# Prefetch depth of a three-chunk product, and the order of its last group and stores

## The chip, the cores and the metric

The kernel runs on one core of a Trainium2 chip. The metric is the device time of one execution in microseconds: 1948.6 us, the median of three runs (1947.58 to 1950.29).

## The reference

One decoder layer on 512 tokens of width 2048, all in float32. The part around the change is the last line, a SwiGLU block of hidden width 5632 and the residual:

```python
    h2 = rms_norm(x, norm2_g[l])
    x = x + (jax.nn.silu(h2 @ w_gate[l]) * (h2 @ w_up[l])) @ w_down[l]
```

Ahead of it the layer has a combined projection, gated linear attention on four heads, dilated attention on eight heads, and an output projection.

## The kernel before

Every large product is computed with Strassen's scheme in Winograd's form on blocks of 256: four quarters a, b, c, d of a 512-row slab of the weights, seven products P1, P5, P6, P3, P7, P2, P4 in that order, each with one of seven combinations of the activation (A11, S1, S2, S4, S3, A12, A22). A product over a group of 512 rows of the weights is an item of the loop in `stream` (L380), called a group below. Each operand is kept as a high part, rounded to the matmul's type by ScalarE, and a low part, the rest, subtracted by VectorE. So a group is twelve matmuls (L398): eight with the weights' high part `wh` (the activation's high and low part, two halves jj of the rows, two halves m of the output rows) and four with the low part `wl`. The two halves m go to two accumulators `acc`. `wh` is cast by ScalarE (L371), `wl` by VectorE (L375), each one group ahead in two buffers; the sums of weight quarters are VectorE's too (L296).

The down product takes the gated activation's 22 blocks in three chunks i = 0, 1, 2 of four, four and three groups of rows. For each chunk there are two column pairs (np_ = 0, 1), each with 7 x 4 or 7 x 3 groups. Chunk 0 adds to `x1_d`, the others to `y_d`, in DRAM; chunk 2 stores to the output. This is `final_down`: the closing sums are made by VectorE (L334), then `residual` loads the rows to be added into the two tiles q and k (L1235) and adds them (L1240, or L1237 where the accumulator itself is still the source, as for the last two tiles of a pair).

The activation's parts of the next chunk are split while the second column pair of the chunk before runs. `down_jobs` makes the list of parts (28, or 21 for the last chunk) in the order of the products, each a load of 256 KB from `p_d` (a gated block, transposed) or from `sums_d` (sums of such blocks, printed S_d) into a tile, and a split into a tile of `apool`: a copy by ScalarE (L196) and a subtraction by VectorE (L197). `staged` keeps a number of loads ahead of the split in hand, and each step of the pair, one per group, splits one part. `fetch_part` gives the loads the tiles v, T, qT and kT in turn. The tiles oT and PT hold, until the end of the layer's gate and up product, the transposed gated tiles on their way to `p_d`.

Most loads and stores are issued by SP, which works through its queue in order and waits there for what an entry needs. The order of that queue is not that of the code: a scheduler places each instruction by when it expects its operands. TensorE, VectorE and ScalarE are each in order as well.

Of the kernel before, what the change touches and what calls it, by code (L numbers as in the profile page):

```python
# [14 lines left out]
ALU = mybir.AluOpType  # L15
# [3 lines left out]
P = 128  # L19
# [112 lines left out]
def block_kernel(ctx: ExitStack, tc: tile.TileContext, ins, out):  # L132
    nc = tc.nc
# [18 lines left out]
    def nm(s):  # L152
        uid[0] += 1
        return f"{s}_{uid[0]}"
# [7 lines left out]
    def work(tag, shape=(P, 512), bufs=1):  # L162
        return mp.tile(list(shape), F32, name=nm(tag), tag=tag, bufs=bufs)
# [6 lines left out]
    load = nc.sync.dma_start  # L170
    store = nc.sync.dma_start
# [88 lines left out]
    def folded(w):  # L260

        return w.rearrange("p (b a) -> p a b", b=2)

    def unfolded(t):

        return t.rearrange("p (a b) -> p b a", b=2)

    def halves(t):
        return t.rearrange("p (b a) -> p b a", b=2)
# [88 lines left out]
    def stream(pairs):  # L358


        items = [(p, prod, g) for p in pairs for prod in PRODUCTS for g in range(p.op.groups)]
        last = len(items) - 1
        sources, high, low = {}, {}, {}

        def total(k):
            p, prod, g = items[k]
            sources[k] = p.source(prod, g)

        def first_part(k):
            high[k] = hpool.tile([P, 2, 512], F32R, name=nm("wh"), tag="wh")  # L370
            nc.scalar.copy(high[k], sources[k])  # L371

        def second_part(k):
            low[k] = hpool.tile([P, 2, 512], F32R, name=nm("wl"), tag="wl")
            nc.vector.tensor_tensor(  # L375
                low[k], sources.pop(k), high[k].bitcast(F32), op=ALU.subtract
            )

        yield total, first_part, second_part
        for k, (p, prod, g) in enumerate(items):  # L380
            if g == 0:
                if prod == "P1" and p.before:
                    p.before()
                p.begin(prod)
            run_soon()
            if k < last:
                first_part(k + 1)
            if k + 2 <= last:
                total(k + 2)
            if k < last:  # L390
                second_part(k + 1)
            a = p.op.t[COMBO[prod], g]
            fresh = prod in ("P1", "P5", "P2")
            for w, terms in ((high.pop(k), (0, 1)), (low.pop(k), (0,))):
                for jj in range(2):
                    for m in range(2):
                        for hl in terms:
                            nc.tensor.matmul(  # L398
                                p.dst[prod][m], a[:, jj, hl, m * P : (m + 1) * P], folded(w[:, jj, :]),
                                start=fresh and g == 0 and len(terms) == 2 and jj == 0 and hl == 0,  # L400
                                stop=g == p.op.groups - 1 and len(terms) == 1 and jj == 1,
                                skip_group_check=not fresh,
                            )
                if len(terms) == 2:
                    p.step()
            if g == p.op.groups - 1:
                p.end(prod)
# [7 lines left out]
    def run_soon():  # L415
        for d in list(soonest):
            d[0] -= 1
            if d[0] <= 0:
                soonest.remove(d)
                d[1]()  # L420
# [267 lines left out]
    for g in range(4):  # L688
        for b in (2 * g, 2 * g + 1):
            if g < 2:  # L690
                t = apool.tile([P, 2, 512], F32, name=nm("xT"), tag="A")
# [342 lines left out]
    order = (2, 3, 0, 1)  # L1034
# [92 lines left out]
    def staged(items, ahead=1):  # L1127

        queue = []
        for key, fetch, use in items:  # L1130
            while key is not None and key not in done:
                if queue:
                    t, u = queue.pop(0)
                    u(t)
                yield
            queue.append((fetch(), use))
            if len(queue) > ahead:
                t, u = queue.pop(0)
                u(t)
                yield  # L1140
        for t, u in queue:
            u(t)
            yield

    tags = ("v", "T", "qT", "kT")
    count = [0]

    def fetch_part(src, half):
        def fetch():
            t = work(tags[count[0] % 4], (P, 2, 256))  # L1150
            count[0] += 1
            load(t, src[half])
            return t

        return (id(src), half), fetch
# [74 lines left out]
    def residual(tiles, acc_, rows, c0, src):  # L1230

        res = []
        for m in range(2):
            r = work(("q", "k")[m])
            load(r, src(rows[m], c0))  # L1235
            if tiles is None:
                nc.vector.tensor_tensor(halves(r), unfolded(acc_[m]), halves(r), op=ALU.add)  # L1237
                res.append(r)
            else:
                nc.vector.tensor_tensor(tiles[m], tiles[m], r, op=ALU.add)  # L1240
                res.append(tiles[m])
        return res
# [121 lines left out]
    def sums_job(j):  # L1364
# [19 lines left out]
        put("S4", v)  # L1384
        yield

    opd = [Operand(4), Operand(4), Operand(3)]

    def down_jobs(i):

        op = opd[i]
        items = []
        for prod in PRODUCTS:
            name = COMBO[prod]
            for g in range(op.groups):
                j = 4 * i + g
                if name in SUMS:
                    src = (sums_d[j][name], 0)
                else:
                    src = (p_d[2 * j + (name != "A11")], int(name == "A22"))  # L1400
                items.append(
                    (*fetch_part(*src), lambda t, name=name, g=g: op.split(name, g, t))
                )
        return staged(items, 2)

    paces = {0: [1, 1, 1, 1, 0, 0, 0, 0, 0, 0, 1, 1, 1, 1, 0, 0, 0, 0], 10: [0] * 6}
    def before_ffn(j):
        if j == 0:
            finish(lambda: ("A11", 3) in opn.t)
        elif j == 10:  # L1410
            background.append(down_jobs(0))
# [10 lines left out]
    def final_down(i, np_):  # L1422
        def final(half, which, tiles, acc_):
            rows = [2 * half, 2 * half + 1]
            c0 = 512 * (2 * np_ + which)
            prev = x1_d if i == 0 else y_d
            tiles = residual(tiles, acc_, rows, c0, lambda t, c: prev[t][:, c : c + 512])
            for m in range(2):
                t = rows[m]
                if i == 2:  # L1430
                    store(out[t * P : (t + 1) * P, c0 : c0 + 512], tiles[m])
                else:
                    store(y_d[t][:, c0 : c0 + 512], tiles[m])

        return final

    for i in range(3):
        g0 = 4 * i
        rows_d = [(512 * (g0 + g), 512 * (g0 + g) + 256) for g in range(opd[i].groups)]
        for np_ in range(2):  # L1440
            lead = np_ == 1 and i < 2
            pair(
                opd[i], rows_d, w_down[:, 2 * np_], w_down[:, 2 * np_ + 1],
                final_down(i, np_), paced([0] * 6) if lead else step,
                before=(lambda i=i: background.append(down_jobs(i + 1))) if lead else None,
            )

    rest = stream(pairs)
    begin = next(rest)
    with tc.manual_schedule(engines=ordered):  # L1450
# [57 lines left out]
```

## Time and profile before

| What | Value |
|---|---|
| median of the runs | 1948.6 us (1947.58 to 1950.29) |
| the profiled execution, own time | 1952.11 us |
| its span, first to last instruction | 1950.0 us |
| granted TensorE clock, mean | 0.998 |
| TensorE busy | 1916.9 us (98%) |
| VectorE busy | 1647.6 us (84%) |
| ScalarE busy | 1088.9 us (56%) |
| DMA, mean over the span | 178 GB/s |

Rows of the trace in order of time give the start in us from the span's start, the length, the engine (PE is TensorE, PEld its weight loads, DVE VectorE, ACT ScalarE, SPq the issue of a DMA by SP), the line, the operation, what is written and read by the program's names, and how many instructions of that kind stand together. Brackets give the idle time ahead of the row and what ended it. Ends of matmuls are modelled. Rows of windows give the stretch, the busy time and count for PE, PEld, DVE, ACT and POOL, the granted clock, the share of the DMA engines and GB/s. Rows of DMA issues end with the size of one and the median time to landing.

### The profile page before, as it was taken

The numbers are of one execution on the slowest core, as the hardware profiler recorded it, in microseconds if no ns is written. First come the engines' busy times: TensorE is split into PE (matmuls) and PEld (weight loads), VectorE is DVE, ScalarE is ACT, GpSimd is POOL, SyncE is SP. The second block draws the span as 40 slices with busy tenths as digits, with TensorE's granted clock in tenths as the row PEclk, the third lists the DMA queues.
The fourth block names the chain that finished last, engine by engine and source line by source line (L and its number), as shares of the span: only waits on it lengthen the run. The fifth ranks groups of instructions, "written<-read, shape, count | busy, mean of one in ns | idle before, by whom it ended". The sixth has DMA issues, their size and how long they took to land.

```text
span 1950.0 us, 25512 instructions
## 1 busy us (share of the span) xinstructions
PE 1916.9 (98%) x9160; PEld 1660.6 (85%) x9160; DVE 1647.6 (84%) x1845; ACT 1088.9 (56%) x1580; POOL 47.2 (2%) x73
## 2 busy tenths in 40 slices
PE   7999999999999999999999999999999999999998
PEld 6788888887888888888888888888888888888887
DVE  7996877767799999878878878878879989989987
ACT  8654564566676675544544544544546646546443
POOL 0000230001000000000000000000000000000000
PEclk9999999999999999999999999999999999999999
DMA  9445555454535563454464454453555765855662
GB/s 354 170 151 205 171 189 154 149 164 150 176 138 186 184 224 117 138 178 162 135 189 148 144 184 137 155 184 121 171 172 180 270 217 177 292 195 180 235 216 76
DMA packets 150791, 347.84 MB, mean 178 GB/s; under 512 B 15542, under 2 KB 42463, under 8 KB 150664
## 3 DMA queue, kind: packets, MB, share of 16 engines
q1 hardware_dynamic: 150520, 346.21, 53.5%
q8 instruction: 71, 1.16, 0.2%
q14 instruction: 56, 0.46, 0.1%
q10 hardware_dynamic: 144, 0.01, 0.0%
HBM read 288.20 MB, written 60.31 MB: 179 GB/s over the span
## 4 chain that ended last, share of the span: by engine, by line
PE 72%; DVE 7%; DMA 3%; issue 2%; ACT 1%; SPq 0%; POOLq 0%; POOL 0%; DVEq 0%; ACTq 0%
PE acc L398 68%; DVE wl L375 3%; PE bank L1059 1%; DVE wa L296 1%; PE bank L944 1%; PE bank L968 1%; DVE AS L197 1%; DMA wc<-in_w_in 0%; DMA p_d<-PT 0%; PE bank L935 0%; PE bank L961 0%; ACT wh L371 0%; DMA r<-p_d 0%; ACT jk L1019 0%; DMA q<-in_x 0%
## 5 line engine op out<-in xcount | busy, mean ns | idle before, releaser
L398 PE MATMUL acc<-wh,AS 128*128 128x512 f32 x3008 | 711.1, 379 | 0.0
L398 PEld LDWEIGHTS acc<-wh,AS 128*128 128x128 f32 x3008 | 568.6, 189 | 81.1 <-ACT wh L371 0.4
L371 ACT CAST wh<-wa 128x1024 fp32r<-128x1024 f32 x376 | 394.2, 1049 | 397.8 <-PE acc L398 357.7
L398 PE MATMUL acc<-wh,AA 128*128 128x512 f32 x2256 | 533.7, 379 | 2.8 <-ACT wh L371 2.8
L375 DVE TENSOR_TENSOR wl<-wa,wh 128x1024 fp32r<-128x1024 f32 x376 | 457.2, 1218 | 68.0 <-ACT wh L371 42.2
L398 PEld LDWEIGHTS acc<-wh,AA 128*128 128x128 f32 x2256 | 426.0, 189 | 64.5 <-ACT wh L371 4.0
L398 PE MATMUL acc<-wl,AS 128*128 128x512 f32 x1504 | 396.3, 385 | 3.9 <-DVE wl L375 3.8
L398 PEld LDWEIGHTS acc<-wl,AS 128*128 128x128 f32 x1504 | 280.1, 189 | 55.4 <-DVE wl L375 13.6
L398 PE MATMUL acc<-wl,AA 128*128 128x512 f32 x1128 | 295.1, 384 | 0.0
L398 PEld LDWEIGHTS acc<-wl,AA 128*128 128x128 f32 x1128 | 210.0, 189 | 29.8 <-issue 1.0
L371 ACT CAST wh<-wb 128x1024 fp32r<-128x1024 f32 x94 | 98.5, 1048 | 124.0 <-PE acc L398 118.4
L371 ACT CAST wh<-wc 128x1024 fp32r<-128x1024 f32 x94 | 98.5, 1047 | 110.8 <-PE acc L398 106.5
L371 ACT CAST wh<-wd 128x1024 fp32r<-128x1024 f32 x94 | 98.6, 1049 | 101.9 <-PE acc L398 93.3
L375 DVE TENSOR_TENSOR wl<-wc,wh 128x1024 fp32r<-128x1024 f32 x94 | 114.6, 1220 | 41.0 <-ACT wh L371 41.0
L375 DVE TENSOR_TENSOR wl<-wd,wh 128x1024 fp32r<-128x1024 f32 x94 | 114.4, 1219 | 38.9 <-ACT wh L371 30.1
L296 DVE TENSOR_TENSOR wa<-wc,wa 128x1024 f32<-128x1024 f32 x94 | 114.4, 1220 | 34.0 <-DMA wc<-in_w_gate 20.6
L375 DVE TENSOR_TENSOR wl<-wb,wh 128x1024 fp32r<-128x1024 f32 x94 | 114.1, 1217 | 4.8 <-ACT wh L371 4.5
L296 DVE TENSOR_TENSOR wa<-wb,wa 128x1024 f32<-128x1024 f32 x94 | 113.6, 1219 | 1.1 <-DMA wb<-in_w_in 0.4
L296 DVE TENSOR_TENSOR wb<-wd,wb 128x1024 f32<-128x1024 f32 x94 | 114.1, 1217 | 0.4
L296 DVE TENSOR_TENSOR wa<-wd,wa 128x1024 f32<-128x1024 f32 x94 | 113.0, 1217 | 0.8 <-DMA wd<-in_w_in 0.8
L338 DVE SCALAR_TENSOR_TENSOR seed<-acc,rs,seed 128x512 f32<-128x512 f32 x96 | 70.3, 745 | 27.8 <-PE acc L398 27.8
L322 ACT ACTIVATE seed<-acc,rs 128x512 f32<-128x512 f32 x96 | 60.7, 683 | 4.1 <-PE acc L398 4.1
(301 smaller groups left out, 1323.7 us busy)
## 6 DMA issues: line engine op xcount, KB each, us to landing
wa<-in_w_gate SPq DMA_DIRECT2D x44, 512.0 KB, 3.4
wb<-in_w_up SPq DMA_DIRECT2D x44, 512.0 KB, 4.4
wd<-in_w_up SPq DMA_DIRECT2D x44, 512.0 KB, 4.2
wc<-in_w_gate SPq DMA_DIRECT2D x44, 512.0 KB, 3.5
wc<-in_w_in SPq DMA_DIRECT2D x28, 512.0 KB, 3.5
wa<-in_w_in SPq DMA_DIRECT2D x24, 512.0 KB, 4.8
wb<-in_w_in SPq DMA_DIRECT2D x24, 512.0 KB, 5.9
wd<-in_w_in SPq DMA_DIRECT2D x24, 512.0 KB, 5.6
```

Of the source, the lines that this page charges most:

```text
L197: nc.vector.tensor_tensor(a[:, :, 1, :], src, a[:, :, 0, :].bitcast(F32), op=ALU.subtract)
L296: nc.vector.tensor_tensor(src, other, src, op=ALU.subtract)
L322: nc.scalar.activation(halves(t), unfolded(src[m]), AF.Copy, scale=self.scale(half, m))
L338: nc.vector.scalar_tensor_tensor(halves(seed[m]), unfolded(src[m]), self.scale(half, m), halves(seed[m]), op0=ALU.mult, op1=ALU.add,)
L371: nc.scalar.copy(high[k], sources[k])
L375: nc.vector.tensor_tensor(low[k], sources.pop(k), high[k].bitcast(F32), op=ALU.subtract)
L398: nc.tensor.matmul(p.dst[prod][m], a[:, jj, hl, m * P : (m + 1) * P], folded(w[:, jj, :]), start=fresh and g == 0 and len(terms) == 2 and ...
L944: nc.tensor.matmul(lp[:, :n], qh[:, b * P : (b + 1) * P], kh[:, :n], start=True, stop=True)
L968: nc.tensor.matmul(op, vh[:, k, :], lgs[b][:, k * P : (k + 1) * P], start=(k == 0), stop=(k == b))
L1059: nc.tensor.transpose(bk[:, jj, m * P : (m + 1) * P], tiles[m][:, f : f + P], ident)
```

## The change

Three things are changed; the third has two parts.

1. For chunks 1 and 2 the parts are loaded into six tiles in turn (oT and PT besides the four), with four loads ahead of the split in hand and not two. Chunk 0 stays as it was.
2. In the last group of the program the twelve matmuls are sorted by the half m: all six of the first accumulator, then all six of the second.
3. The last two tiles of the output get their rows in tiles of their own (tag L, two buffers) and no longer in q and k. The second of them is added and stored in two halves of 256 columns; the first of these stores is issued by ScalarE.

```diff
@@ stream
-            for w, terms in ((high.pop(k), (0, 1)), (low.pop(k), (0,))):
-                for jj in range(2):
-                    for m in range(2):
-                        for hl in terms:
-                            nc.tensor.matmul(
-                                p.dst[prod][m], a[:, jj, hl, m * P : (m + 1) * P], folded(w[:, jj, :]),
...
-                if len(terms) == 2:
+            w = high.pop(k), low.pop(k)
+            order = [(i, m, jj, hl) for i in range(2) for jj in range(2) for m in range(2)
+                     for hl in range(2 - i)]
+            if k == last:
+                order.sort(key=lambda o: o[1])
+            for n, (i, m, jj, hl) in enumerate(order):
+                nc.tensor.matmul(
+                    p.dst[prod][m], a[:, jj, hl, m * P : (m + 1) * P], folded(w[i][:, jj, :]),
...
+                if n == 7:
                     p.step()
@@ fetch_part
-    def fetch_part(src, half):
+    def fetch_part(src, half, tags=tags):
         def fetch():
-            t = work(tags[count[0] % 4], (P, 2, 256))
+            t = work(tags[count[0] % len(tags)], (P, 2, 256))
@@ down_jobs
+    wide = tags + ("oT", "PT")
...
-                    (*fetch_part(*src), lambda t, name=name, g=g: op.split(name, g, t))
+                    (*fetch_part(*src, tags if i == 0 else wide), lambda t, name=name, g=g: op.split(name, g, t))
...
-        return staged(items, 2)
+        return staged(items, 2 if i == 0 else 4)
@@ final_down
+            if i == 2 and np_ == 1 and tiles is None:
+                rs = [work("L", bufs=2) for _ in range(2)]
+                for m in range(2):
+                    load(rs[m], prev[rows[m]][:, c0 : c0 + 512])
+                for m in range(2):
+                    for b in range(1 if m == 0 else 2):
+                        c = slice(256 * b, 512 if m == 0 else 256 * b + 256)
+                        src, r = unfolded(acc_[m]), halves(rs[m])
+                        if m == 1:
+                            src, r = src[:, b], r[:, b]
+                        nc.vector.tensor_tensor(r, src, r, op=ALU.add)
+                        (nc.scalar.dma_start if m == 1 and b == 0 else store)(
+                            out[rows[m] * P : (rows[m] + 1) * P, c0 + c.start : c0 + c.stop],
+                            rs[m][:, c],
+                        )
+                return
```

What it moves, in the queues. SP's queue in the second column pair of chunk 0, before: loads of parts stand as v, T, qT, kT from S3_d (block 4 + g) and p_d, loads of weights as wa, the stores of a closed tile as y_d, and the loads of the rows for the next as q and k.

```order
L1152 DMA T_2607_14206<-S3_d5_201 128x512
L257 DMA wa_2628_14315<-in_w_down 128x1024
L1152 DMA qT_2611_14228<-S3_d6_205 128x512
L257 DMA wa_2633_14338<-in_w_down 128x1024
L257 DMA wa_2640_14363<-in_w_down 128x1024
L1433 DMA y_d0_222<-seed_2559_13979 128x512
L1433 DMA y_d1_223<-seed_2564_14002 128x512
L1235 DMA q_2605_14198<-x1_d2_142 128x512
L1235 DMA k_2606_14201<-x1_d3_143 128x512
L1152 DMA kT_2615_14250<-S3_d7_209 128x512
L1152 DMA v_2619_14273<-p_d9_165 128x512
```

The same place of SP's queue in the changed kernel:

```order
L1154 DMA PT_2609_14210<-S3_d7_209 128x512
L257 DMA wa_2630_14319<-in_w_down 128x1024
L1154 DMA v_2613_14232<-p_d9_165 128x512
L257 DMA wa_2635_14342<-in_w_down 128x1024
L257 DMA wa_2642_14367<-in_w_down 128x1024
L1452 DMA y_d0_222<-seed_2561_13983 128x512
L1452 DMA y_d1_223<-seed_2566_14006 128x512
L1237 DMA q_2607_14202<-x1_d2_142 128x512
L1237 DMA k_2608_14205<-x1_d3_143 128x512
L1154 DMA T_2617_14254<-p_d11_167 128x512
L1154 DMA qT_2621_14277<-p_d13_169 128x512
```

The load of S3_d7 stood behind the stores and the loads of q and k; it now stands ahead of them, in the slot that S3_d5 had, and every later part's load has moved up by two in the same way. In chunk 1's second column pair it is alike: there the load of p_d19 into kT (group 1 of A22) stood behind such stores and loads, and now stands two loads earlier. Where the six tiles start, SP's queue at the end of the gate and up product has a new entry: after the two stores of the last gated tile (p_d20 from oT, p_d21 from PT) the load of p_d8 into oT, and behind it the four loads of r for the last sums.

TensorE's last group (the names are the two accumulators, the weights' high and low part, and the activation's part), before:

```order
L398 MATMUL acc_2947_16022<-wh_3013_16405,AA22_2869_15569 128x512 x2
L398 MATMUL acc_2948_16023<-wh_3013_16405,AA22_2869_15569 128x512 x2
L398 MATMUL acc_2947_16022<-wh_3013_16405,AA22_2869_15569 128x512 x2
L398 MATMUL acc_2948_16023<-wh_3013_16405,AA22_2869_15569 128x512 x2
L398 MATMUL acc_2947_16022<-wl_3014_16407,AA22_2869_15569 128x512
L398 MATMUL acc_2948_16023<-wl_3014_16407,AA22_2869_15569 128x512
L398 MATMUL acc_2947_16022<-wl_3014_16407,AA22_2869_15569 128x512
L398 MATMUL acc_2948_16023<-wl_3014_16407,AA22_2869_15569 128x512
```

and in the changed kernel, with the row ahead of it:

```order
L400 MATMUL acc_2948_16023<-wl_3012_16390,AA22_2865_15548 128x512
L400 MATMUL acc_2947_16022<-wh_3013_16405,AA22_2869_15569 128x512 x4
L400 MATMUL acc_2947_16022<-wl_3014_16407,AA22_2869_15569 128x512 x2
L400 MATMUL acc_2948_16023<-wh_3013_16405,AA22_2869_15569 128x512 x4
L400 MATMUL acc_2948_16023<-wl_3014_16407,AA22_2869_15569 128x512 x2
```

The first accumulator is complete after the sixth matmul and not after the eleventh. The loads of the rows for the last two tiles, in the changed kernel's SP queue at the end of chunk 1 (out of the tiles q and k the stores to y_d, then the rows of the first tiles of chunk 2, and L the new ones):

```order
L1452 DMA y_d2_224<-q_2878_15610 128x512
L1452 DMA y_d3_225<-k_2879_15613 128x512
L1237 DMA q_2921_15865<-y_d0_222 128x512
L1433 DMA L_3017_16442<-y_d2_224 128x512
L1237 DMA k_2922_15868<-y_d1_223 128x512
L1433 DMA L_3018_16443<-y_d3_225 128x512
```

Before, those loads stood near the end of SP's queue, behind the last stores of closed tiles and ahead of the two final stores. On the other engines the order of all instructions is unchanged up to VectorE's last add, which is now two.

More of the change, by code (lines that the diff above doesn't have):

```diff
@@ L393, in stream @@
             fresh = prod in ("P1", "P5", "P2")
-            for w, terms in ((high.pop(k), (0, 1)), (low.pop(k), (0,))):
-                for jj in range(2):
-                    for m in range(2):
-                        for hl in terms:
-                            nc.tensor.matmul(
-                                p.dst[prod][m], a[:, jj, hl, m * P : (m + 1) * P], folded(w[:, jj, :]),
[L400 to L403, printed above, removed]
-                if len(terms) == 2:
+            w = high.pop(k), low.pop(k)
[6 more added lines that the diff above has]
+                    p.dst[prod][m], a[:, jj, hl, m * P : (m + 1) * P], folded(w[i][:, jj, :]),
+                    start=fresh and g == 0 and i == 0 and jj == 0 and hl == 0,
+                    stop=g == p.op.groups - 1 and i == 1 and jj == 1,
+                    skip_group_check=not fresh,
+                )
+                if n == 7:
                     p.step()
@@ L1426, in final @@
             prev = x1_d if i == 0 else y_d
+            if i == 2 and np_ == 1 and tiles is None:
[12 more added lines that the diff above has]
+                            rs[m][:, c],
+                        )
+                return
             tiles = residual(tiles, acc_, rows, c0, lambda t, c: prev[t][:, c : c + 512])
```

## The prediction

> **What bounds the kernel now.** I read the page first, then the instructions in order of time over the down product, then waits and windows. Its first part names TensorE:
>
> ```profile
> PE 1916.9 (98%) x9160; PEld 1660.6 (85%) x9160; DVE 1647.6 (84%) x1845; ACT 1088.9 (56%) x1580; POOL 47.2 (2%) x73
> ```
>
> So gains can only come from places where TensorE waits, and from what follows its last matmul. An undisturbed group of twelve matmuls takes 2.59 us from start to start (1665.68 to 1668.27 below). Twice in the down product a group starts over a microsecond late. TensorE at the first place (start, length; in brackets the idle time and what ended it):
>
> ```profile
> 1665.68 1.89 PE L398 MATMUL acc<-wh,AA 128*128 128x512 f32 x8
> 1668.27 1.89 PE L398 MATMUL acc<-wh,AA 128*128 128x512 f32 x8
> 1672.32 1.99 PE L398 MATMUL acc<-wh,AA 128*128 128x512 f32 x8 [1.25 <-ACT wh L371]
> ```
>
> The third group is due at 1668.27 + 2.59 = 1670.86; it starts 1.46 late and is 0.10 longer than the others: **1.56 us**. The other engines there:
>
> ```profile
> 1654.27 0.32 SPq L1152 DMA_DIRECT2D T<-S_d  x1
> 1664.88 0.43 SPq L1152 DMA_DIRECT2D kT<-S_d  x1
> 1669.79 1.28 DVE L334 TENSOR_TENSOR seed<-acc,seed 128x512 f32<-128x512 f32 x2
> 1670.70 0.62 ACT L196 CAST AS<-kT 128x512 fp32r<-128x512 f32 x1 [4.72 <-DMA kT<-S_d]
> 1670.99 0.68 DVE L1240 TENSOR_TENSOR seed<-seed,q 128x512 f32<-128x512 f32 x1
> 1672.30 1.23 DVE L375 TENSOR_TENSOR wl<-wc,wh 128x1024 fp32r<-128x1024 f32 x1 [0.62 <-ACT wh L371]
> 1680.65 0.63 ACT L196 CAST AA<-kT 128x512 fp32r<-128x512 f32 x1 [2.66 <-DMA kT<-p_d]
> ```
>
> ScalarE was free for the split of part kT at 1670.70 - 4.72 = 1665.98, but SP issued its load only at 1664.88, after the stores and loads that stand ahead of it in its queue, and it took 5.7 us. The cast for the next weights (wh) stands behind that split on ScalarE, so TensorE and VectorE waited for both. The second place is alike, in the next chunk:
>
> ```profile
> 1801.10 0.32 SPq L1152 DMA_DIRECT2D T<-p_d  x1
> 1815.10 1.89 PE L398 MATMUL acc<-wh,AA 128*128 128x512 f32 x8
> 1817.39 0.62 ACT L196 CAST AA<-kT 128x512 fp32r<-128x512 f32 x1 [4.59 <-DMA kT<-p_d]
> 1817.82 0.68 DVE L1240 TENSOR_TENSOR seed<-seed,q 128x512 f32<-128x512 f32 x1
> 1818.99 1.23 DVE L375 TENSOR_TENSOR wl<-wc,wh 128x1024 fp32r<-128x1024 f32 x1 [0.49 <-ACT wh L371]
> 1819.01 1.99 PE L398 MATMUL acc<-wh,AA 128*128 128x512 f32 x8 [1.12 <-ACT wh L371]
> 1829.89 1.22 DVE L375 TENSOR_TENSOR wl<-wa,wh 128x1024 fp32r<-128x1024 f32 x1 [0.85 <-ACT wh L371]
> ```
>
> Due at 1817.69, started at 1819.01, again 0.10 longer: **1.42 us**. The end of the program, with an earlier accumulator for comparison:
>
> ```profile
> 1935.82 1.03 PE L398 MATMUL acc<-wl,AA 128*128 128x512 f32 x4
> 1936.67 0.69 DVE L334 TENSOR_TENSOR seed<-acc,seed 128x512 f32<-128x512 f32 x1 [0.93 <-PE acc L398]
> 1940.20 1.22 DVE L375 TENSOR_TENSOR wl<-wa,wh 128x1024 fp32r<-128x1024 f32 x1
> 1940.71 0.45 SPq L1235 DMA_DIRECT2D q<-y_d  x1
> 1941.86 1.89 PE L398 MATMUL acc<-wh,AA 128*128 128x512 f32 x8
> 1943.59 1.03 PE L398 MATMUL acc<-wl,AA 128*128 128x512 f32 x4
> 1945.07 0.69 DVE L1237 TENSOR_TENSOR q<-acc,q 128x512 f32<-128x512 f32 x1 [3.64 <-DMA q<-y_d]
> 1945.80 0.69 DVE L1237 TENSOR_TENSOR k<-acc,k 128x512 f32<-128x512 f32 x1
> 1946.52 0.34 SPq L1431 DMA_DIRECT2D out<-k  x1
> SPq L1504 <- DMA out<-k: 2.0, 1, 2.0
> ```
>
> VectorE starts on a finished accumulator 0.18 before the modelled end of its last matmul (1936.85 against 1936.67), so the first closing add could start at 1943.59 + 1.03 - 0.18 = 1944.44. It starts at 1945.07, since its rows were loaded only at 1940.71. The last store, issued at 1946.52, has landed by 1946.86 + 2.0 = 1948.86 (the last row, from the waits of SP's queue); the span ends 1.14 later.
>
> **The change part by part.** Four parts ahead. TensorE's, VectorE's and ScalarE's orders stay as they were up to the last group; only SP's order moves, so nothing else is added to their queues. Each load takes the slot that the load of the part two before it had: at the first place S3_d7 goes out near 1654.27 and not at 1664.88, at the second p_d19 near 1801.10. By the 5.7 us above they land some 6 and 10 us before their splits. Next in danger is p_d11, now in the slot of 1664.88: landing about 1670.6, while its split is due two groups after 1665.98, at 1671.16. That is 0.5 us of cover; if it is gone, little is lost at first, since ScalarE's wait of 2.66 us at 1680.65 above held up no matmul. So both ScalarE waits go. What is late next is VectorE, which was busy without a break:
>
> ```profile
> 1644.94 1.22 DVE L375 TENSOR_TENSOR wl<-wd,wh 128x1024 fp32r<-128x1024 f32 x1
> 1646.21 1.13 PE L398 MATMUL acc<-wl,AS 128*128 128x512 f32 x4
> 1711.44 1.22 DVE L375 TENSOR_TENSOR wl<-wa,wh 128x1024 fp32r<-128x1024 f32 x1
> 1713.00 1.03 PE L398 MATMUL acc<-wl,AS 128*128 128x512 f32 x4
> 1716.87 1.23 DVE L375 TENSOR_TENSOR wl<-wd,wh 128x1024 fp32r<-128x1024 f32 x1 [0.81 <-ACT wh L371]
> ```
>
> Its low part (wl) ends at 1646.16, the four matmuls on it start 0.05 later and take 1.13 where others take 1.03: a late wl costs its lateness + 0.05 + 0.10. At the first place wl can follow the add of 1670.99 by one step of 0.60 (two adds take 1.28, of which 0.68 is the second): 1671.59 to 1672.81. TensorE wants it 1.73 after the group's start (1941.86 to 1943.59), at 1672.59. The loss is 0.22 + 0.15 = 0.37, the gain 1.56 - 0.37 = 1.19. From there VectorE runs 0.71 earlier than before (1671.59 for 1672.30) but TensorE 1.19, so every wl has 0.48 less room. The thinnest in that stretch is at 1713.00: wl ended at 1712.66, 0.34 ahead. It becomes 0.14 too late, a loss of 0.29. From 1716.87 VectorE waits for ScalarE again and nothing more is lost. First place: **0.90**. Second: wl at 1817.82 + 0.60 to 1819.64, wanted at 1817.69 + 1.73 = 1819.42, loss 0.37, gain **1.05**; VectorE is idle again by 1829.89. Bounds: nothing, if the loads are late again, to the full 1.56 and 1.42. I take the worked values, since VectorE's rows leave no other start.
>
> The six tiles add one wait: oT and PT still hold the last gated tile, so SP must see oT's store land before it loads p_d8 there; four loads of r, and the sums on VectorE, stand behind it.
>
> ```profile
> 1552.08 1.74 SPq L1122 DMA_DIRECT2D r<-p_d  x4
> 1558.01 1.22 DVE L375 TENSOR_TENSOR wl<-wa,wh 128x1024 fp32r<-128x1024 f32 x1
> 1559.88 1.03 PE L398 MATMUL acc<-wl,AS 128*128 128x512 f32 x4
> 1650.00:1672.00 22.00, 21.06 (x98) 17.75 (x96) 21.67 (x26) 10.96 (x15) 0.00 (x0) 1.00 0.92 304
> ```
>
> Those loads waited for PT's store, issued after oT's, already; added are one issue (1.74 / 4 = 0.44) and 256 KB on the DMA engines, 0.86 us at the 304 GB/s of the last row. VectorE may be up to 1.3 us late, against 0.65 of room in wl (1559.23 to 1559.88): a loss between 0 and 1.3 - 0.65 + 0.15 = 0.8. I take 0, since SP's old wait for PT's store covers the new one, and keep 0.8 for the range.
>
> The end. The rows' loads now go out behind the stores of the chunk before, two column pairs of 21 groups or 2 x 21 x 2.59 = 109 us earlier. With the last group sorted by row half, the first accumulator is done after six of its twelve matmuls, and its add (0.69) and store lie beside the other six. wl is ready at 1941.42 and is now wanted after four matmuls (4 x 1.73 / 8 = 0.86), at 1942.72. Six matmuls in a row go to one bank; sixteen did, at 1.8 / 15 = 0.12 us for half the columns, no slower than 0.216 for the whole:
>
> ```profile
> L741 PE MATMUL bank<-AS,gs x16: 274/281/283, 60.3 to 62.1; 128*128 128x256 f32 x16
> L834 DVE SCALAR_TENSOR_TENSOR L<-bank,L 128x256 f32<-128x256 f32 x4 | 1.6, 410 | 0.0
> ```
>
> The second accumulator is added in halves of 128x256, 0.41 us by the last row: 1944.44 to 1944.85, and 1944.77 to 1945.18. SP issues the last half 0.03 later, at 1945.21 for 1946.52: **1.31**. It lands and closes as before. Unsplit, the add would have ended at 1945.13, so the split gains nothing by itself; the first half's issue on ScalarE lies beside the second add. Bounds: 0.63 (the rows' load alone) to 1.37 (a split that costs nothing).
>
> [...]
>
> **Sum.** 0.90 + 1.05 + 1.31 = 3.26 us of the profiled execution, whose span is 1950.0 and own time 1952.11. The median of the runs is 1948.6, 3.5 below that; I take the same microseconds off it: **1945.3**.
>
> **The rivals.** First, VectorE keeps up (it finds slack that the rows hide): 1.56 + 1.42 + 1.31 = 4.29, 1944.3. Against it stand its rows without a gap. Second, the two waits are not there to be saved, because loads land sooner in runs without the profiler's traffic, or the moved loads are late in the stretch where the DMA engines are 0.92 busy: only the end is won, 1947.3. The 3.5 us between profile and median speak for it, two alike stalls in one execution against it. Third, slower: the first half's store goes by ScalarE's queue, unused since the program's start. If it lands as slowly as the slowest 256 KB store of the trace, the program's end waits for it:
>
> ```profile
> va<-seed SPq DMA_DIRECT2D x6, 256.0 KB, 8.2
> ```
>
> Issued at 1944.85 it lands at 1953.05, the end is 1954.19, and less 1.95 for the two places that is 2.2 slower: 1950.8. It decides once it takes longer than 1948.86 + 1.95 - 1944.85 = 6.0 us. Against it: the DMA engines are nearly idle then, and SP's last store took 2.34.
>
> **How the numbers follow.** My sum 0.45, VectorE keeps up 0.25, end only 0.20, ScalarE's store 0.06, other losses 0.04. About 0.2% or 3.9 us is what a measurement of this kernel can tell from no change, and my sum lies just inside. With 0.7 us of scatter on it, faster by more takes 0.20 of the second case and 0.14 of the first: 0.34; slower by more, half of the last two: 0.05; within: 0.61. The range leaves out most of the slow cases and reaches below the full gain by the scatter: 1943.2 to 1947.9.
>
> **What would show it.** Right: no group of the down product waits for ScalarE's split; the groups at the two places are 0.3 to 0.4 late after wl, not 1.3 to 1.5; one near 1711 is late by 0.3; the last store is issued 1945.21 - 1941.86 = 3.35 us after the last group's first matmul, not 4.66. Wrong: ScalarE waiting for p_d11 or its followers, VectorE waiting for r near 1556, or a program end that waits for ScalarE's store.

## The result

The changed kernel takes 1946.18 us (median of 14 runs, 1941.98 to 1950.16) against 1950.36 (14 runs, 1946.55 to 1953.33) before. The ratio is 0.9977 with a 95% interval of 0.9968 to 0.9985: 0.23% faster, or 4.5 us (2.9 to 6.2) of 1950. The forecast was 3.3 us, inside that interval. Ratios leave out one run of e5 (2885.76 us) and two of the kernel before beside it (2510.14 and 4119.75), far above all others. The profiled execution has an own time of 1947.03 and a span of 1945.25, 4.72 below the 1949.97 of before: 0.66 of it ahead of the down product (its first group starts at 1538.49 for 1539.15, where the change moves nothing; over all profiles below that start lies between 1536.9 and 1541.6), 2.62 in fewer waits of TensorE in the down product, 1.44 behind the last group's first matmul.

The first part of the changed kernel's page; TensorE is now busy for 99% of the span:

```profile
PE 1917.8 (99%) x9160; PEld 1662.6 (85%) x9160; DVE 1647.6 (85%) x1846; ACT 1088.5 (56%) x1580; POOL 47.7 (2%) x73
```

The first place in the changed kernel, in order of time (start, length; a bracket would give a wait and what ended it). The load of S3_d7 is now the one into PT:

```profile
1652.51 0.32 SPq L1154 DMA_DIRECT2D PT<-S_d  x1
1664.12 0.62 ACT L196 CAST AS<-PT 128x512 fp32r<-128x512 f32 x1
1669.23 0.68 DVE L1242 TENSOR_TENSOR seed<-seed,q 128x512 f32<-128x512 f32 x1
1669.39 0.62 ACT L196 CAST AA<-T 128x512 fp32r<-128x512 f32 x1
1669.83 1.22 DVE L375 TENSOR_TENSOR wl<-wc,wh 128x1024 fp32r<-128x1024 f32 x1
1671.10 1.13 PE L400 MATMUL acc<-wl,AA 128*128 128x512 f32 x4
1672.07 1.89 PE L400 MATMUL acc<-wh,AA 128*128 128x512 f32 x8
```

The load goes out at 1652.51 and the split of PT runs at 1664.12 with no bracket, so without a wait. Nor does the next in danger, p_d11 (T, at 1669.39), have one. VectorE's add ends, wl follows by 0.60, ends at 1671.05, and its matmuls start 0.05 later and take 1.13: the next group is 0.35 late, where one was 1.46 and the next 0.10 late before. Near 1703 and 1711, and at the second place:

```profile
1702.29 1.13 PE L400 MATMUL acc<-wl,AS 128*128 128x512 f32 x4
1710.24 1.13 PE L400 MATMUL acc<-wl,AS 128*128 128x512 f32 x4
1812.74 0.61 ACT L196 CAST AA<-oT 128x512 fp32r<-128x512 f32 x1
1815.77 1.21 DVE L375 TENSOR_TENSOR wl<-wc,wh 128x1024 fp32r<-128x1024 f32 x1
1817.04 1.13 PE L400 MATMUL acc<-wl,AA 128*128 128x512 f32 x4
```

The two rows of 1.13 make their next groups 0.11 and 0.18 late. At the second place the split of p_d19 (oT, 1812.74) does not wait, and the group behind 1817.04 is 0.35 late, for 1.42 before. The end:

```profile
1938.58 1.03 PE L400 MATMUL acc<-wh,AA 128*128 128x512 f32 x4
1940.08 0.69 DVE L1440 TENSOR_TENSOR L<-acc,L 128x512 f32<-128x512 f32 x1 [1.93 <-PE acc L400]
1940.74 0.59 PE L400 MATMUL acc<-wl,AA 128*128 128x512 f32 x2
1941.38 0.76 DVE L1440 TENSOR_TENSOR L<-acc,L 128x256 f32<-128x256 f32 x2 [0.60 <-PE acc L400]
1941.83 0.35 ACTq L1441 DMA_DIRECT2D out<-L  x1
1942.16 0.33 SPq L1441 DMA_DIRECT2D out<-L  x1
```

and from the waits of SP's queue there (total, times, longest):

```profile
SPq L1523 <- DMA out<-L: 1.6, 3, 0.7
```

The first accumulator's add lies beside the second's matmuls, the second's two half adds start 0.05 behind the last matmul, and the last store is issued 3.58 us after the last group's first matmul (4.66 before). SP's longest last wait for a store is 0.7, where it was 2.0, and the span ends 3.09 after the last issue (3.45 before). So of the 1.44 us of the end 1.08 come from the earlier issue and 0.36 from what follows it.

### The profile page after: what moved, and what is told of

Read it like the earlier page. It is cut to its first block, busy times and chain, and to the rows that moved or that the text cites. A ratio compares the mean times of both kernels' runs of the same rounds, so it can differ in the third digit from the quotient of the medians.

```text
span 1945.2 us, 25510 instructions
## 1 busy us (share of the span) xinstructions
PE 1917.8 (99%) x9160; PEld 1662.6 (85%) x9160; DVE 1647.6 (85%) x1846; ACT 1088.5 (56%) x1580; POOL 47.7 (2%) x73
## 4 chain that ended last, share of the span: by engine, by line
PE 82%; DVE 10%; issue 3%; DMA 3%; ACT 2%; SPq 0%; POOL 0%; POOLq 0%; DVEq 0%; ACTq 0%
PE acc L400 75%; DVE wl L375 3%; PE acc L463 1%; DVE wa L296 1%; PE bank L1061 1%; DVE AS L197 1%; PE bank L946 1%; PE bank L970 1%; DVE wl L515 1%; PE bank L463 0%; DMA wc<-in_w_in 0%; PE bank L937 0%; ACT wh L371 0%; PE bank L963 0%; DVE AS L209 0%
```

## The experiments

Each ratio is to the kernel before, run beside it on the same chip; e1, e2, e3 and e6 shared one chip and its runs of before, so did e4, e5, e8 and e9, and e10 to e13. Lateness means: by how much more than 2.59 us two groups of TensorE are apart. Groups are counted from 0, the down product's first. "Place 1" sums groups 49 to 68 (from about 1668 to 1717), "place 2" groups 105 to 110 (1815 to 1829), "start" the groups 30 to 47 at the start of chunk 0's second column pair, "rows" groups 135 to 146 (about 1890 to 1920), "end" is the time from the last group's first matmul to the end of the span.

| Profile | place 1 | place 2 | start | rows | end |
|---|---|---|---|---|---|
| before | 1.56 | 1.42 | 1.25 | 1.02 | 8.11 |
| e1, before again | 2.62 | 0.37 | 0.14 | 2.87 | 8.31 |
| e3, end alone | 4.54 | 1.40 | 0.15 | 2.65 | 6.63 |
| changed | 0.64 | 0.35 | 0.14 | 1.44 | 6.67 |
| e10, changed again | 0.62 | 0.35 | 0.53 | 1.58 | 6.62 |
| e2, parts alone | 0.63 | 0.34 | 0.14 | 2.29 | 8.64 |
| e6, two ahead | 0.64 | 0.34 | 0.14 | 2.10 | 6.65 |
| e4, unsplit | 0.63 | 0.34 | 0.47 | 2.50 | 6.86 |
| e5, rows alone | 0.64 | 0.34 | 0.15 | 1.92 | 7.62 |
| e8, more rows | 0.63 | 0.34 | 0.15 | 0 | 6.62 |
| e11, rows all | 0.63 | 0.34 | 0.14 | 0 | 6.67 |

**e1, the kernel before again** (no edit).

> The kernel before, once more, to see which of its waits come back in a second execution. If the two late splits are set by the order of SP's queue, ScalarE waits again for the loads of S3_d7 and p_d19 and two groups of the down product again start 1.3 to 1.5 us late; if they are chance, they are elsewhere or gone. The five groups that were 0.1 to 0.3 late between 1628 and 1650 follow a wait of VectorE of 1.01 for the rows in q, which the changed kernel's profile does not have: by chance it differs between executions, so at least one of the five places differs here; if the change removed it, all of them (1.25 us) come back. Time: the same as before, within 0.15%.

Measured: ratio 0.9995 (0.9985 to 1.0005).

```profile
1663.30 0.43 SPq L1152 DMA_DIRECT2D kT<-S_d  x1
1669.53 0.62 ACT L196 CAST AS<-kT 128x512 fp32r<-128x512 f32 x1 [5.17 <-PE acc L398]
1671.15 1.99 PE L398 MATMUL acc<-wh,AA 128*128 128x512 f32 x8 [1.71 <-ACT wh L371]
1810.92 0.44 SPq L1152 DMA_DIRECT2D kT<-p_d  x1
1815.70 0.62 ACT L196 CAST AA<-kT 128x512 fp32r<-128x512 f32 x1 [3.46 <-DMA kT<-p_d]
1817.34 2.00 PE L398 MATMUL acc<-wh,AA 128*128 128x512 f32 x8
```

Both late splits are there again, so they belong to the order of SP's queue; what they cost is not fixed. The first split runs 6.23 us after its load's issue and TensorE is 1.91 late (the split's bracket names TensorE, whose group had just ended; but in the other two profiles with four tiles the same split waits for the load, and in the changed kernel it runs before that group starts, so it was the load). A third split waits 3.51 us at 1690.69 and costs 0.44, and with 0.27 in two more groups it is 2.62 in all. At the second place the split runs 4.78 us after the load's issue and TensorE lost only 0.37. The 1.25 us of the "start" column did not come back: those were chance, and no part of the change (e10 and e4, with the change, have some of them).

**e2, the parts alone**

```diff
-            if k == last:
+            if False:
                 order.sort(key=lambda o: o[1])
...
-            if i == 2 and np_ == 1 and tiles is None:
+            if False:
```

> The first of the three changes alone (six tiles, four ahead). My sum: the two late splits are gone, VectorE's low part is 0.35 late at both places and 0.29 near 1711, so TensorE's waits fall by 1.95 us; the end stays at 8.1 us from the last group's first matmul to the end of the span. Time 0.10% below before. The rival that VectorE keeps up: 2.98 us, 0.15%. The rival that only the end is won: no change in time.

Measured: ratio 0.9987 (0.9977 to 0.9996), 0.13% or 2.5 us. The interval is no judge between my sum (0.10%) and the rival that VectorE keeps up (0.15%); it excludes no gain. The profile decides between the two: the lateness behind wl is there, at 0.34, 0.29 and 0.34.

**e3, the end alone**

```diff
-    wide = tags + ("oT", "PT")
+    wide = tags
...
-        return staged(items, 2 if i == 0 else 4)
+        return staged(items, 2)
```

> The second and third change alone (sorted last group, own rows, last tile in halves). My sum: from the last group's first matmul to the end of the span 1.3 to 1.5 us less than the 8.1 before, and the two late splits are there as before. Time 0.07% below before. If only the end is won by the change, this kernel has all of it: 0.23% below before.

Measured: ratio 0.9986 (0.9977 to 0.9995), 0.14% or 2.7 us; 0.23%, all of the change, is at the interval's end. The end takes 6.63. The first place is the worst of the three profiles with four tiles:

```profile
1665.59 0.51 SPq L1154 DMA_DIRECT2D kT<-S_d  x1
1672.53 0.62 ACT L196 CAST AS<-kT 128x512 fp32r<-128x512 f32 x1 [6.11 <-DMA kT<-S_d]
1674.15 3.59 PE L400 MATMUL acc<-wh,AA 128*128 128x512 f32 x8 [2.64 <-ACT wh L371]
1675.87 0.68 DVE L197 TENSOR_TENSOR AS<-kT,AS 128x512 fp32r<-128x512 f32 x1
```

Issued at 1665.59, the part is split only at 1672.53. The group starts 2.84 late and its eight matmuls take 3.59 for 1.89: half of them need the part's own low part, which VectorE, late too, subtracts at 1675.87. That is 4.54 us at one place, from one load whose split came 1.1 us later than in the first profile (6.94 after its issue, for 5.82).

**e6, six tiles, two ahead**

```diff
-        return staged(items, 2 if i == 0 else 4)
+        return staged(items, 2)
```

> The changed kernel with two loads ahead instead of four, but the six tiles kept. SP's order is then that of the changed kernel except for one load that moves by one entry, so if the place in SP's queue is what matters, the two late splits stay away and the time is that of the changed kernel (0.23% below before, within 0.1%). If the number of loads in hand matters, the splits are late again, two groups wait 1.3 to 1.5 us, and the time is about 0.07% below before.

Measured: ratio 0.9966 (0.9954 to 0.9979), from five runs. In the profile the two places are those of the changed kernel:

```profile
1671.70 1.13 PE L400 MATMUL acc<-wl,AA 128*128 128x512 f32 x4
1672.66 1.89 PE L400 MATMUL acc<-wh,AA 128*128 128x512 f32 x8
1818.60 1.46 PE L400 MATMUL acc<-wh,AA 128*128 128x512 f32 x6
```

So it is the six tiles that bring the loads forward. The number in hand changes nothing at the two places: it shifts the load in the code, but SP's order is set by when the tile comes free, and that order is the changed kernel's but for this one load. (The reverse, more in hand with four tiles, was not run; its SP order has the load of S3_d7 behind the stores as before.)

**e4, the last tile whole**

```diff
-                    for b in range(1 if m == 0 else 2):
-                        c = slice(256 * b, 512 if m == 0 else 256 * b + 256)
+                    for b in range(1):
+                        c = slice(0, 512)
...
-                        (nc.scalar.dma_start if m == 1 and b == 0 else store)(
+                        store(
```

> The changed kernel, with the last tile added and stored whole, by SP. My step says that the split into column halves gains nothing by itself: the whole add takes 0.69 and not 0.76 for two halves, so the last store is issued 0.05 to 0.1 us earlier, and from there to the end of the span it takes the same 3.0 us. By the size of the store, half the bytes should land sooner: then the end here is 0.3 us later than in the changed kernel (6.6 us from the last group's first matmul to the end). Time the same as the changed kernel's within noise; the profile decides.

Measured: ratio 0.9976 (0.9967 to 0.9985), which can't be told from the changed kernel's.

```profile
1940.93 1.03 PE L400 MATMUL acc<-wh,AA 128*128 128x512 f32 x4
1943.72 0.69 DVE L1438 TENSOR_TENSOR L<-acc,L 128x512 f32<-128x512 f32 x1 [0.60 <-PE acc L400]
1944.44 0.33 SPq L1439 DMA_DIRECT2D out<-L  x1
```

```profile
SPq L1521 <- DMA out<-L: 1.9, 1, 1.9
```

The last store is issued 3.51 after the last group's first matmul, 0.07 sooner than with the split, as my step had it; but it ends the span 3.35 later and not 3.09. SP waits 1.9 for it. A half store is over 0.26 sooner, so the split gains 0.2. The same holds over all profiles: 3.04 to 3.09 us from the last issue to the end of the span in the nine with a half store, 3.35 to 3.73 in the five with a whole one. So of the two expected values the one by the store's size is the nearer.

**e5, only the rows' tiles of the end**

```diff
-            if k == last:
+            if False:
                 order.sort(key=lambda o: o[1])
```

with e4's edit besides.

> Of the end only the rows' own tiles, loaded early: the last group in its old order, both tiles added and stored whole by SP. My lower bound: the first add starts 0.63 us earlier after the last group than before, since it no longer waits for its rows, and the end is 7.5 us after the last group's first matmul, between 8.1 before and 6.6 in the changed kernel. If the rows' wait were the whole of it, it would be 6.6 to 6.8.

Measured: ratio 0.9987 (0.9975 to 1.0000).

```profile
1942.17 1.89 PE L400 MATMUL acc<-wh,AA 128*128 128x512 f32 x8
1944.75 1.29 DVE L1438 TENSOR_TENSOR L<-acc,L 128x512 f32<-128x512 f32 x2 [3.01 <-PE acc L400]
```

The adds start 2.58 after the group (3.21 before): 0.63, the forecast's lower bound. The end takes 7.62. With e4 that divides the end: mean of the three profiles with the old end 8.35 (they lie between 8.11 and 8.64); own rows 0.73 less; the order by row half 0.76 less (7.62 to 6.86); the split 0.2 less.

**e8, own rows for two tiles more**

```diff
-            if i == 2 and np_ == 1 and tiles is None:
+            if i == 2 and tiles is None:
```

and the split and ScalarE's store kept to `np_ == 1`.

> The changed kernel, with own row tiles for the last two tiles of chunk 2's first column pair as well. In the changed kernel VectorE waits 1.69 us for q's rows at 1887.66 and four groups from 1893 to 1913 are 0.26, 0.50, 0.50 and 0.18 us late. If that wait is their cause, it goes and the four fall from 1.44 to at most 0.5 us, time 0.05% below the changed kernel. If VectorE's work there is too much anyway, they stay above 1.0.

Measured: ratio 0.9974 (0.9963 to 0.9984). The groups near 1893 are all on time in the profile. Their cause in the other profiles is one row, here of e1:

```profile
1891.19 0.69 DVE L1237 TENSOR_TENSOR q<-acc,q 128x512 f32<-128x512 f32 x1 [3.44 <-DMA q<-y_d]
1893.07 1.13 PE L398 MATMUL acc<-wl,AA 128*128 128x512 f32 x4 [1.15 <-DVE wl L375]
```

VectorE waits 3.44 us for q's rows and everything behind it, the next low part first, is late. In the nine profiles of the table without such tiles this add waits 1.59 (before) to 3.44 us (e1) and 1.0 to 2.9 us are late there, least and most in the same two; in the two with them nothing. (For the add of before and of e5 the bracket names TensorE; that the rows are the cause there is taken from the others.) The intervals of e4 and e8, from the same chip, overlap.

**e9, adds on GpSimd**

```diff
-    def residual(tiles, acc_, rows, c0, src):
+    def residual(tiles, acc_, rows, c0, src, eng=nc.vector):
...
-                nc.vector.tensor_tensor(tiles[m], tiles[m], r, op=ALU.add)
+                eng.tensor_tensor(tiles[m], tiles[m], r, op=ALU.add)
...
-            tiles = residual(tiles, acc_, rows, c0, lambda t, c: prev[t][:, c : c + 512])
+            tiles = residual(tiles, acc_, rows, c0, lambda t, c: prev[t][:, c : c + 512],
+                             nc.gpsimd if i < 2 and np_ == 1 else nc.vector)
```

> The changed kernel, with the adds of rows to closed sums in the second column pairs of chunks 0 and 1 on GpSimd, which is 2% busy, and not on VectorE. If VectorE is what binds at the two places now, the groups that are 0.35 late at 1672 and 1818 and the two of 0.11 and 0.18 near 1703 and 1711 are on time, 1.0 us less. If the low part is late for another reason (ScalarE's cast of the high part), they stay. A price may come with it: SP's stores of the sums wait for GpSimd, and with them the loads behind; if an add there takes over 3 us, splits get late again and the time is above the changed kernel's.

Measured: ratio 1.0002 (0.9992 to 1.0012). All of the gain is gone.

```profile
1661.03 1.29 POOL L1242 TENSOR_TENSOR seed<-seed,q 128x512 f32<-128x512 f32 x1 [1193.27 <-DMA v<-p_d]
1661.32 2.08 DVE L375 TENSOR_TENSOR wl<-wb,wh 128x1024 fp32r<-128x1024 f32 x1
1662.27 2.27 POOL L1242 TENSOR_TENSOR seed<-seed,k 128x512 f32<-128x512 f32 x1
1663.33 1.78 DVE L197 TENSOR_TENSOR AS<-T,AS 128x512 fp32r<-128x512 f32 x1
1665.62 1.21 DVE L296 TENSOR_TENSOR wa<-wc,wa 128x1024 f32<-128x1024 f32 x1
1666.76 1.21 DVE L375 TENSOR_TENSOR wl<-wb,wh 128x1024 fp32r<-128x1024 f32 x1
1668.03 1.13 PE L400 MATMUL acc<-wl,AS 128*128 128x512 f32 x4 [1.71 <-DVE wl L375]
```

VectorE's low part takes 2.08 beside the add on GpSimd (1.22 alone), its next subtraction 1.78 (0.68 alone), and TensorE waits 1.71 for a low part. Three groups at the first place and three at the second are 0.61, 1.97, 0.22 and 0.51, 1.97, 0.23 late. The time was lost, but not by the way that I named: no split waits for its load here. The order of VectorE's work has changed too: the scheduler has put a sum of weights (wa, 1665.62) ahead of the low part that is due (1666.76). e13 below has the same order on VectorE, ScalarE and TensorE without any add, and there these six groups are 1.25 late in all and not 5.5; so the order makes the group behind it late, but the loss against the changed kernel comes with the adds on GpSimd. Both lengths are roughly those of an instruction that has waited for the add beside it: 2.08 against 1.22 plus the 1.00 (1661.03 + 1.29 - 1661.32) that was left of the first add when the low part began, 1.78 against 0.68 plus the 1.21 (1662.27 + 2.27 - 1663.33) that was left of the second when the subtraction began. Why they would wait is not shown.

**e10, the changed kernel again** (no edit).

> The changed kernel once more, beside the three below on the same chip. If the loads are early enough in every execution, the two places read as in its first profile: one group 0.35 late near 1672, 0.29 in two groups near 1703 and 1711, one 0.35 late near 1818, and none waits for ScalarE there. The end takes 6.6 us from the last group's first matmul. The groups late near 1893 differ (they hang on the rows in q): 1.4 to 2.9 us. Time 0.23% below before, within 0.1%.

Measured: ratio 0.9980 (0.9970 to 0.9990); the two places within 0.02 of the first profile's, "rows" 1.58, the end 6.62.

**e11, own rows at every pair's end**

```diff
-            if i == 2 and np_ == 1 and tiles is None:
+            if tiles is None:
+                last = i == 2 and np_ == 1
...
-                            out[rows[m] * P : (rows[m] + 1) * P, c0 + c.start : c0 + c.stop],
+                            (out[rows[m] * P : (rows[m] + 1) * P, c0 + c.start : c0 + c.stop]
+                             if i == 2 else y_d[rows[m]][:, c0 : c0 + 512]),
```

and the split and ScalarE's store under `last`.

> The changed kernel, with own row tiles, loaded early, for the last two tiles of every column pair of the down product and not of the last alone. If late rows are what makes VectorE wait where a pair ends, the groups late near 1893 (1.4 to 2.9 us in the profiles so far) are all on time, and none of the groups from 1612 to 1645 is late (0 to 1.25 us); the 0.35, 0.29 and 0.35 stay. Time 0.05 to 0.15% below the changed kernel's. If VectorE's work there is too much by itself, the groups stay late by about 1.4 us and the time is the same.

Measured: ratio 0.9966 (0.9954 to 0.9979), seven runs, median 1946.47 beside 1948.60 for e10.

```profile
1886.87 0.68 DVE L1441 TENSOR_TENSOR L<-acc,L 128x512 f32<-128x512 f32 x1
1887.90 1.03 PE L400 MATMUL acc<-wl,AA 128*128 128x512 f32 x4
```

No bracket: the rows are there, and no group is late from 1890 on. With e8 that settles the cause of the "rows" column. "Start" is 0.14, as low as the best. This is the fastest version, by 2.1 us of medians; its interval and e10's still touch, so the time alone does not show it.

**e12, the half store by SP**

```diff
-                        (nc.scalar.dma_start if m == 1 and b == 0 else store)(
+                        store(
```

> The changed kernel, with the first half of the last tile stored by SP and not by ScalarE. By my step the issue on ScalarE only lies beside the second half's add: on SP it takes 0.34 us and ends about when that add ends, so the last store is issued 0 to 0.3 us later and the end takes 6.6 to 6.9 us. By the rival that ScalarE's store lands slowly and holds the end, the end is shorter than 6.6 here.

Measured: ratio 0.9979 (0.9969 to 0.9989), the end 6.71.

```profile
1936.96 1.03 PE L400 MATMUL acc<-wh,AA 128*128 128x512 f32 x4
1940.20 0.33 SPq L1441 DMA_DIRECT2D out<-L  x1
1940.63 0.39 SPq L1441 DMA_DIRECT2D out<-L  x1
```

The last store is issued 3.67 after the last group's first matmul, 0.09 later than in the changed kernel. ScalarE's issue is worth 0.1 at most and its store holds up nothing.

**e13, the adds left out**

```diff
-                nc.vector.tensor_tensor(tiles[m], tiles[m], r, op=ALU.add)
+                if add:
+                    nc.vector.tensor_tensor(tiles[m], tiles[m], r, op=ALU.add)
...
-            tiles = residual(tiles, acc_, rows, c0, lambda t, c: prev[t][:, c : c + 512])
+            tiles = residual(tiles, acc_, rows, c0, lambda t, c: prev[t][:, c : c + 512],
+                             i == 2 or np_ == 0)
```

> The changed kernel without the twelve adds of rows to closed sums in the second column pairs of chunks 0 and 1 (what they would add to the output is missing; their rows are still loaded, earlier). It takes 1.2 us of VectorE's work away at each closing and puts it on no other engine. If VectorE is what binds at the two places, the groups 0.35 late near 1672 and 1818 and the 0.29 near 1703 and 1711 are on time, about 1.0 us less. If ScalarE's cast or the loads bind there, they stay.

Measured: ratio 0.9975 (0.9964 to 0.9985). The 0.35, 0.29 and 0.35 are gone, but two other groups, 0.09 late in the changed kernel, are 0.62 late near 1667 and 0.63 near 1812:

```profile
1660.95 1.21 DVE L375 TENSOR_TENSOR wl<-wb,wh 128x1024 fp32r<-128x1024 f32 x1
1662.09 0.68 DVE L197 TENSOR_TENSOR AS<-T,AS 128x512 fp32r<-128x512 f32 x1
1663.29 1.22 DVE L296 TENSOR_TENSOR wa<-wc,wa 128x1024 f32<-128x1024 f32 x1
1664.42 1.21 DVE L375 TENSOR_TENSOR wl<-wb,wh 128x1024 fp32r<-128x1024 f32 x1
1665.69 1.13 PE L400 MATMUL acc<-wl,AS 128*128 128x512 f32 x4 [0.35 <-DVE wl L375]
```

Without the adds the scheduler has put a sum of weights (wa, 1663.29) ahead of the low part that is due; in the changed kernel it stands behind that, at 1665.76. The six groups were 1.17 late together and are 1.25. So VectorE binds here, as TensorE waits for its low part in both, but how late that comes hangs on the order of VectorE's work and not on its sum alone. The expected gain of 1.0 us did not come. The first two rows are those that took 2.08 and 1.78 in e9, in the same order.

## Why the prediction was right

**The mechanism of the loads** held: the two ScalarE waits, for S3_d7 and p_d19, are gone in every profile with six tiles and there in every one with four. That the place in the queue, given by the tiles, does it, and not the four ahead that headed my step, is e6.

**What is late next** held within 0.02: 0.37, 0.29 and 0.37 forecast, 0.35, 0.29 and 0.35 measured. The 0.29 came in two groups, 0.11 and 0.18, where I had one. VectorE's rows left no other start, and the rival that it keeps up (a quarter of my chances) falls in all profiles.

**The cover of p_d11**, 0.5 us by my working, does not always hold. In five of the eleven profiles with six tiles its split waits for the load, by 0.08 to 0.56 us, the most in e8:

```profile
1668.54 0.62 ACT L196 CAST AA<-T 128x512 fp32r<-128x512 f32 x1 [0.56 <-DMA T<-p_d]
```

I had named ScalarE waiting for p_d11 as a sign of being wrong. It cost nothing: the lateness of place 1 is 0.62 to 0.64 in these as in the table's others with six tiles, so little was lost when the cover went, as my step had it.

**The size of the stalls removed** was the weak term. I took 1.56 and 1.42 from one execution; three executions with four tiles give 1.56, 2.62 and 4.54 at the first place and 1.42, 0.37 and 1.40 at the second. Their means, 2.91 and 1.06, less the 0.63 and 0.35 that stay, are 2.28 and 0.71, or 3.0 us where I had 1.95 (three executions are few for a mean). That the pair of profiles in the result shows 1.99 at the two places is no test of the size: it is the execution of before from which I had taken the stalls. The stall is a race between a load (split 4.8 to 6.9 us after its issue) and ScalarE, and its cost can grow faster than its lateness: a split 1.1 us later (e3) cost 3.0 more.

**The end** was forecast at 1.31 and is 1.44 from profile to profile, 1.7 by the means (8.35 for e1, e2 and before; 6.64 for the six profiles of the table that have all of the new end). My step that the split gains nothing was wrong by 0.2: the span ends 3.09 us after the issue of a half store and 3.35 after that of a whole one (e4). The other way, the add starts 0.05 behind the modelled end of two matmuls and not 0.18 ahead of it, so the last store is issued at 3.58 and not at 3.35.

With 3.0 and 1.7 the sum is 4.7 us; measured are 4.5 (2.9 to 6.2), and 2.5 and 2.7 for the two halves alone.

**The other rivals.** That only the end is won: e2 gains without it. That ScalarE's store is slow: e12. (The 8.2 us that I took there for the slowest store is its row's median; the slowest of them took 10.9. And the DMA engines, which I called nearly idle there, were 0.37 busy from 1942 to 1945 in the changed kernel.) The wait for oT's store ahead of the loads of r, which I bounded by 0 and 0.8 and took at 0, showed as 0.1, 0.26 and 0.1 us in one group near 1560 of e12, e4 and e13, and in no other profile: VectorE waited there 0.5 to 0.7 for r. That oT's store is what delayed r there is not shown.

The change lies at the edge of what can be told from no change, as forecast; that it came out just above 0.2% and not just inside fits the 1.0 us by which the two places together were undersized, and the 0.4 of the end.

## What to carry to other kernels

A wait that one profile shows at a load has a price that differs from execution to execution (here 1.6 to 4.5 us at one place, 0.4 to 1.4 at another); its cause can be read from one profile, its size cannot. When a stall goes, the engine behind it can be computed from the old trace: place its instructions end to end from the new start and compare with when their results are due. Here a deeper prefetch in the code, four loads for two, moved one load by one entry of the queue, and the tile count set the places of the others; count buffers first.

## What the runs showed of the hardware that was not expected

Beside two adds of 128x512 on GpSimd (1.29 and 2.27 us) two instructions of VectorE took longer: 2.08 for 1.22, 1.78 for 0.68 (e9). Half a store of 256 KB ended the span 0.26 us sooner after its issue than a whole one (3.09 for 3.35, the changed kernel and e4).
